# Modulation vectors from raw float32 panels: the conditioning becomes the moving operand

## The chip, the cores and the metric

The kernel runs on one core of a Trainium2 chip. The metric is the device time of one execution in microseconds. The engines of the core work side by side and are kept in step by semaphores: TensorE (PE, its weight loads PEld), VectorE (DVE), ScalarE (ACT), GpSimd (POOL) and SyncE (SP), which issues the transfers here.

## The reference, cut to what matters

Two layers of a diffusion backbone work on 640 tokens, 128 of a prompt and 512 latents. Every layer begins with six modulation vectors of 1024 channels, for the prompt's conditioning and for the latents' apart:

```python
mod = jnp.dot(jax.nn.silu(cvec), w_mod[l]) + b_mod[l]          # w_mod[l]: 1024 x 6144
sh1, sc1, g1, sh2, sc2, g2 = jnp.split(mod[:, None, :], 6, axis=-1)
h = rmsnorm(x, norm1[l]) * (1 + sc1) + sh1
u = h @ w_in[l]                # convolution, recurrence and attention read u; their merge is m
x = x + g1 * (m @ w_out[l])
h2 = rmsnorm(x, norm2[l]) * (1 + sc2) + sh2
...                            # a gated feed-forward on h2, added with g2
```

`cvec` is a row of 1024 numbers; there are two of them, so a vector is a product of 2 x 1024 by 1024 x 1024. All numbers are float32.

## The kernel before, in words

Channels lie on the 128 partitions, tokens along the free axis. The large products need nearly all of float32: weights and activations are split into two parts that the faster format fp32r holds exactly, and three products are summed (`gemm`, L268, for halves of 256 and 384 tokens; `gemm_tm`, L279). A panel of weights (128 x 2048 float32, 1 MB) is loaded into one of two places of `rawt`, which take turns (`load_raw`, L239); `split_cols` makes the parts, a copy on ScalarE (L249) and a subtraction on VectorE (L250), into one of four places of `wR`.

Of layer 0, five vectors are made on TensorE by `modulation` (L356 to L380); the last of layer 0 and all of layer 1 are made on VectorE (`mod_vectors`), which the change leaves alone. A vector has four panels. Each is split like other weights, in two halves. The split conditioning lies in `cpad` with zeros around it, so that a load of 8 columns of it yields 8 rows of results: two parts for two conditionings, for either half of the channels. The panel's parts then move past it, 512 columns a product (L369), 32 products a vector, all summed in one bank of PSUM. ScalarE copies the 8 x 512 sums out (L372), TensorE turns them in four steps (L374), VectorE adds the parts (L376, L379), and `mod_finish` adds the bias and scales (L387 to L392).

Two vectors, 1 and then 0, are made at the program's start; their panels have four places of their own (`stage`). Vector 1 is made first, then come the loads of the stream `x` (L1174, eight tiles of 128 x 640) with the sums of squares (`SqSum`: squares L460 on ScalarE, sums L461 on VectorE), then vector 0. `make_h` turns the sums into 1 / rms (`stat_rstd`: products with ones, L318, five calls for the two halves of the tokens; then turned back, L327) and writes `h` in two parts (L477, L479 on VectorE, L478 on ScalarE), which all products of the layer read. Vectors 2, 3 and 4 are made beside the recurrence of layer 0: `spread` puts one step, a panel, behind every third step of the large products there, and `weave` puts these between the recurrence's own products (L778 for its levels).

The code is written step by step; a scheduler orders each engine's instructions by what is ready and by priority. Loads, splits and what empties PSUM (inside `hp`) go ahead of the rest. Each engine then works through its list in order.

Of the kernel before, what the change touches and what calls it, by code (L numbers as in the profile page):

```python
# [10 lines left out]
F32 = mybir.dt.float32  # L11
# [13 lines left out]
# taps of the convolution beside the making of queries and keys, and beside a tile of scores  # L25
# [4 lines left out]
# columns of the parameter pack  # L30
# [5 lines left out]
# columns of the row pack (one layer)  # L36
# [3 lines left out]
class Arena:  # L40
    """Columns of one tile, given out and taken back in program order; the tile's
    own tracking orders the accesses. The part that has been free longest goes first."""
# [51 lines left out]
def tile_trunk_step(  # L94
# [33 lines left out]
    # ---------------------------------------------------------------- storage  # L128
# [5 lines left out]
    cpad = cpool.tile([P, KD, 12], F32R, name="cpad")  # L134
# [35 lines left out]
    def banks(kind):  # L170
        """Banks for the large products; pairs for scores and levels; the rest."""
# [18 lines left out]
        else:  # L190
            gring.use(singles(0, 1, 2, 4, 5))
            wring.use(pairs(6))
            tring.use(pairs(6))
            mring.use(singles(3))
# [3 lines left out]
    # ---------------------------------------------------------------- helpers  # L198
# [12 lines left out]
    def flat(pair):  # L211
        """The first 640 columns of two banks."""
        return pair.rearrange("p b n -> p (b n)")[:, :NT]
# [11 lines left out]
    def next_t():  # L225
        """For what is done with at once."""
        ctr["t"] += 1
        return ur[:, 3 + ctr["t"] % 2]

    def load_raw(src, n, at=None):  # L230
        """One panel of weights: n columns per partition."""
# [10 lines left out]
    def split_cols(raw3):  # L242
        """Weights [128, K, c] into two parts that float32r holds exactly; list over k of (hi, lo)."""
# [16 lines left out]
    def gemm(wk, ak, hf):  # L260
        """sum_k w_k^T a_k for one half of the tokens; the three products that float32 holds."""
# [9 lines left out]
    def gemm_tm(wk, ak, i):  # L271
        """(token tile i of a)^T w; [128, 256]."""
# [9 lines left out]
    def panel8(src):  # L282
        """A panel [128, 8, 256]: two column tiles, each a list over k."""
# [7 lines left out]
    def panel_wide(src, K):  # L291
        """A panel [128, K <= 4, 512]: four column tiles."""
# [8 lines left out]
    def rsqrt(dst, var, n):  # L301
        """dst = var ** -0.5 for var > 0."""
# [9 lines left out]
    def stat_rstd(s, sl, scale, eps, post=None, ring=None):  # L312
        """s: [128 ch, 640] whose column sums are the squares; 1 / rms of the tokens of sl
        on every partition, in a psum bank."""
# [15 lines left out]
    def streams(sl):  # L330
        """The parts of a slice of tokens that belong to the prompt (0) and to the latents (1)."""
# [6 lines left out]
    # ---------------------------------------------------------------- constants  # L338
# [1116 lines left out]
```

## Time and profile before

| | |
|---|---|
| median of 3 runs | 2509.78 us (2509.27 to 2509.84) |
| profiled execution, first to last instruction | 2509.0 us |
| TensorE busy | 2480.4 us, 99% |
| VectorE busy | 1747.9 us, 70% |
| ScalarE busy | 916.8 us, 37% |
| DMA, mean | 100 GB/s |

The execution that was profiled lies 0.8 us below the median of the runs by its span; that is what the span leaves out and the spread of the runs. In a group of instructions the columns are: line, engine, operation, tiles written and read, shape, count; then busy microseconds and the mean nanoseconds of one; then the idle time of the engine before them and what ended it. In a timeline a row is a merged piece: its start, how long it lasts from the first start to the last end, engine, line, operation, count, and in brackets the idle time before it. TensorE's products overlap, so the distance between two of them is the piece's length less the last one's own duration, divided by the count less one. In a table of stretches each engine's busy time and count stand in the order PE, PEld, DVE, ACT, POOL, and then the granted TensorE clock (1.00 is 2.4 GHz, 0.50 is 1.2 GHz), the share of the DMA engines and GB/s. Before the first clock event of an execution, at about 14.5 us here, the column reads 1.00 whatever the clock was.

### The profile page before, as it was taken

To read this page: it belongs to the slowest core of one execution; us is meant where nothing else is said; L and a number is where in the kernel's file an instruction comes from. 1 tells how busy PE (TensorE), PEld (TensorE's weight loads), DVE (VectorE), ACT (ScalarE), POOL (GpSimd) and SP (SyncE) were. 2 spreads that over 40 slices of the span, in tenths; PEclk is the share of its full clock that TensorE was granted. 3 is DMA by queue.
4 is the path that set the end of the run, shared out by engine and by line. 5 is a ranking of instruction groups with operands and counts; after the bars stand their busy time and mean duration, and the time that the engine had idled before them with its cause. 6 is when DMAs were issued, how large, how long until landed. Compare 5 with 4: busy or idle time off the path is not lost.

```text
span 2509.0 us, 41312 instructions
## 1 busy us (share of the span) xinstructions
PE 2480.4 (99%) x17054; PEld 2393.0 (95%) x17054; DVE 1747.9 (70%) x3570; ACT 916.8 (37%) x1741; POOL 2.6 (0%) x28
## 2 busy tenths in 40 slices
PE   6999999999999999999999999999999999999999
PEld 4999889999999999999999998899999999999999
DVE  8587788685778897767685868885667884444343
ACT  5244565544332422222243445543433242222221
POOL 0000000000000000000000000000000000000000
PEclk8999999999999999999999999999999999999999
DMA  6222111432243354343332222012222412221221
GB/s 268 75 86 92 70 57 57 145 131 103 76 159 112 110 182 154 120 149 135 137 110 77 99 80 77 34 63 73 80 83 71 151 68 68 85 85 68 76 77 59
DMA packets 60492, 251.01 MB, mean 100 GB/s; under 512 B 6416, under 2 KB 18448, under 8 KB 37776
## 3 DMA queue, kind: packets, MB, share of 16 engines
q1 hardware_dynamic: 60304, 248.37, 28.5%
q8 instruction: 134, 2.20, 0.4%
q14 instruction: 54, 0.44, 0.1%
HBM read 230.52 MB, written 17.83 MB: 99 GB/s over the span
## 4 chain that ended last, share of the span: by engine, by line
PE 96%; DVE 2%; DMA 1%; ACT 1%; issue 0%; SPq 0%; DVEq 0%; ACTq 0%
PE psum L268 74%; PE psum L279 9%; PE psum L778 3%; PE psum L988 2%; PE psum L1024 2%; PE psum L987 1%; PE psum L369 1%; PE psum L1016 1%; PE psum L819 1%; DVE wR L250 1%; DMA aF<-in_wmod_dram 1%; PE psum L933 0%; PE psum L834 0%; PE psum L318 0%; PE psum L837 0%
## 5 line engine op out<-in xcount | busy, mean ns | idle before, releaser
L268 PE MATMUL psum<-hR,wR 128*128 128x256 f32 (+1 forms) x8832 | 1342.7, 311 | 3.1 <-ACT hR L478 2.1
L268 PEld LDWEIGHTS psum<-hR,wR 128*128 128x128 f32 x8832 | 1301.7, 190 | 10.9 <-issue 4.4
L250 DVE TENSOR_TENSOR wR<-rawt,wR 128x1024 fp32r<-128x1024 f32 x324 | 395.3, 1223 | 346.0 <-ACT wR L249 345.2
L249 ACT CAST wR<-rawt 128x1024 fp32r<-128x1024 f32 x324 | 338.4, 1047 | 785.6 <-PE psum L268 679.6
L268 PE MATMUL psum<-oR,wR 128*128 128x256 f32 (+1 forms) x4032 | 609.5, 310 | 0.3 <-DVE aF L1138 0.3
L268 PEld LDWEIGHTS psum<-oR,wR 128*128 128x128 f32 x4032 | 592.1, 189 | 3.3 <-DVE aF L1138 0.5
L1138 DVE SCALAR_TENSOR_TENSOR aF<-psum,modd,aF 128x128 f32<-128x128 f32 (+1 forms) x432 | 174.1, 435 | 105.0 <-PE psum L268 102.8
L279 PE MATMUL psum<-wR,hR 128*128 128x256 f32 x1920 | 243.0, 285 | 0.0
L279 PEld LDWEIGHTS psum<-wR,hR 128*128 128x128 f32 x1920 | 233.5, 191 | 3.5 <-issue 2.8
L639 DVE SCALAR_TENSOR_TENSOR aF<-aF,pk 128x655 f32<-128x655 f32 x240 | 214.9, 895 | 2.9
L411 DVE CUSTOM_DVE_ANT_0 aF<-aF 128x1024 f32<-128x1024 f32 x112 | 136.6, 1219 | 0.8
L1335 DVE TENSOR_TENSOR ur<-ur,psum 128x256 f32<-128x256 f32 (+1 forms) x88 | 42.9, 487 | 75.5 <-PE psum L268 75.5
L994 DVE TENSOR_REDUCE small<-psum 128x1 f32<-128x640 f32 (+1 forms) x80 | 56.6, 714 | 45.0 <-PE psum L988 41.0
L254 ACT CAST oR<-ur 128x256 fp32r<-128x256 f32 (+2 forms) x96 | 45.8, 479 | 93.9 <-DVE ur L1335 83.8
L778 PE MATMUL psum<-aF 128*128 128x128 f32 x560 | 78.1, 287 | 0.7 <-ACT aF L766 0.7
L778 PEld LDWEIGHTS psum<-aF 128*128 128x128 f32 x560 | 72.2, 191 | 4.3 <-ACT aF L766 1.6
L567 ACT ACTIVATE ur<-psum 128x256 f32<-128x256 f32 (+1 forms) x104 | 45.3, 436 | 72.3 <-PE psum L268 72.1
L766 ACT COPY aF<-aF 128x640 f32<-128x640 f32 x56 | 43.8, 782 | 72.8 <-DVE aF L782 59.6
L997 ACT ACTIVATE aF<-psum,small 128x640 f32<-128x640 f32 (+1 forms) x80 | 56.6, 711 | 25.8 <-DVE small L995 25.6
L255 DVE TENSOR_TENSOR oR<-ur,oR 128x256 fp32r<-128x256 f32 (+2 forms) x96 | 49.3, 515 | 19.7 <-ACT oR L254 19.7
L568 DVE SCALAR_TENSOR_TENSOR ur<-ur,psum 128x256 f32<-128x256 f32 (+1 forms) x104 | 50.2, 483 | 16.6 <-ACT ur L567 16.5
L369 PE MATMUL psum<-wR,cpad 128*8 128x512 f32 x160 | 46.4, 424 | 11.7 <-ACT wR L249 9.9
(170 smaller groups left out, 1761.6 us busy)
## 6 DMA issues: line engine op xcount, KB each, us to landing
rawt<-in_win_dram SPq DMA_DIRECT2D x64, 1024.0 KB, 4.8
rawt<-in_wfi_dram SPq DMA_DIRECT2D x44, 1024.0 KB, 4.7
aF<-in_wmodT_dram SPq DMA_DIRECT2D x28, 1024.0 KB, 4.8
rawt<-in_wfo_dram SPq DMA_DIRECT2D x20, 1024.0 KB, 4.9
rawt<-in_wmod_dram SPq DMA_DIRECT2D x12, 1024.0 KB, 4.8
rawt<-in_wbr_dram SPq DMA_DIRECT2D x24, 512.0 KB, 3.4
aF<-in_wmod_dram SPq DMA_DIRECT2D x8, 1024.0 KB, 10.5
aF<-in_xT_dram SPq DMA_DIRECT2D x16, 320.0 KB, 6.0
```

Source lines behind the costliest of these rows:

```text
L249: S.copy(hi, raw3)
L250: V.tensor_tensor(out=lo, in0=raw3, in1=f32(hi), op=ALU.subtract)
L268: T.matmul(ps, lhsT=w, rhs=a[:, sl], start=k == 0 and q == 0, stop=k == n - 1 and q == 2)
L279: T.matmul(ps, lhsT=a[:, sl], rhs=w, start=k == 0 and q == 0, stop=k == n - 1 and q == 2)
L369: T.matmul(ps, lhsT=cpad[:, k, 4 - 4 * i : 12 - 4 * i], rhs=w, start=i == 0 and k == 0 and j == 0, stop=i == 1 and k == 7 and j == 1)
L411: V.tensor_tensor_reduce(out=out, in0=w[:, q * 1024 : (q + 1) * 1024], in1=cb[s], scale=1.0, scalar=0.0, op0=ALU.mult, op1=ALU.add, accum_ ...
L568: V.scalar_tensor_tensor(out=dst[:, sl], in0=dst[:, sl], scalar=1.0, in1=ps, op0=ALU.add, op1=ALU.mult)
L639: V.scalar_tensor_tensor(out=accs[j], in0=pads[j][:, t : t + CO], scalar=w(j, t), in1=accs[j], op0=ALU.mult, op1=ALU.add)
L778: T.matmul(ps[:, c // 4, (c % 4) * P : (c % 4 + 1) * P], lhsT=kc[:, c * P : (c + 1) * P], rhs=qm[:, c * nc1 : (c + 1) * nc1], start=True, ...
L994: V.tensor_reduce(out=mx[:, c : c + 1], in_=srcs[c], axis=AX.XY, op=ALU.max)
L997: S.activation(e.rearrange("p (h n) -> p h n", h=2 if i else 1), srcs[c], AF.Exp, bias=mx[:, c : c + 1], scale=0.125, accum_out=sm[:, c : ...
L1138: last = V.scalar_tensor_tensor(out=x[:, ss], in0=ps[:, ss.start - sl.start : ss.stop - sl.start], scalar=g[:, s : s + 1], in1=x[:, ss], o ...
```

## The change

The panels are not split any more. `modulation` takes 128 x 128 pieces of the raw float32 panel as the stationary operand and moves the two columns of the raw conditioning `cs` past them: four tiles of channels by four pieces a panel, 16 products, 64 a vector. The result has its channels on the partitions, so copy, turning and adding of parts fall away; the sums of the two halves of the 1024 inputs stand side by side in PSUM and are added by VectorE in `mod_finish`. `cpad` goes. At the start the loads of the stream and their squares come before both vectors, and the two vectors take turns with two banks of PSUM (the large products have four there instead of five). In the recurrence they keep one bank. The steps are whole panels, as before. Comments are gone too; the diff leaves that out.

```diff
-    cpad = cpool.tile([P, KD, 12], F32R, name="cpad")
+    cs = cpool.tile([P, 2 * KD], F32, name="cs")
...
         else:
-            gring.use(singles(0, 1, 2, 4, 5))
+            gring.use(singles(0, 1, 4, 5))
             wring.use(pairs(6))
             tring.use(pairs(6))
-            mring.use(singles(3))
+            mring.use(singles(2, 3))
...
-    V.memset(f32(cpad), 0.0)
-    cs = small(16)
...
-    S.copy(cpad[:, :, 4:6], csv)
-    V.tensor_tensor(out=cpad[:, :, 6:8], in0=csv, in1=f32(cpad[:, :, 4:6]), op=ALU.subtract)
...
     def modulation(l, v, stage=None):
-        bank = mring.next()
-        ps = bank[:8]
-        for i in range(2):
-            for half in range(2):
-                raw = load_raw(wmod[l, 2 * v + i, half], RAW, None if stage is None else stage[2 * i + half])
-                for q in range(2):
-                    wk = split_cols(raw.rearrange("p (k c) -> p k c", c=512)[:, 2 * q : 2 * q + 2])
-                    for kk in range(2):
-                        k = half * 4 + q * 2 + kk
-                        for j, w in enumerate(wk[kk]):
-                            T.matmul(ps, lhsT=cpad[:, k, 4 - 4 * i : 12 - 4 * i], rhs=w, start=i == 0 and k == 0 and j == 0, stop=i == 1 and k == 7 and j == 1)
-                yield
-        ev = next_t()
-        S.copy(ev[:8, :512], ps)
-        for b in range(4):
-            T.transpose(bank[:, b * 8 : (b + 1) * 8], ev[:8, b * P : (b + 1) * P], ident[:8, :8])
-        mt = small(32)
-        V.tensor_copy(mt, bank[:, :32])
-        m4 = mt.rearrange("p (b g r) -> p g b r", b=4, r=4)
-        dst = modt[l][:, 8 * v : 8 * v + 8, :]
-        V.tensor_tensor(out=dst.rearrange("p (g b) s -> p g b s", b=4), in0=m4[:, :, :, 0:2], in1=m4[:, :, :, 2:4], op=ALU.add)
-        mod_finish(l, v)
+        ps = mring.next()[:, :32].rearrange("p (h j s) -> p h j s", h=2, s=2)
+        for i in range(4):
+            n, half = 2 * v + i // 2, i % 2
+            raw = load_raw(wmod[l, n, half], RAW, None if stage is None else stage[i])
+            w = raw.rearrange("p (k c) -> p k c", c=512)
+            for j in range(4):
+                for k in range(4):
+                    T.matmul(ps[:, half, 4 * (i // 2) + j], lhsT=w[:, k, j * P : (j + 1) * P], rhs=csv[:, 4 * half + k], start=k == 0, stop=k == 3)
+            yield
+        mod_finish(l, v, src=ps)
 
-    def mod_finish(l, v, j=0, n=8):
+    def mod_finish(l, v, j=0, n=8, src=None):
         c = 8 * v + j
         dst = modt[l][:, c : c + n, :]
         bm = pkl(l, PK_BMOD + c, n)
+        if src is not None:
+            V.tensor_copy(dst, src[:, 0])
+            V.tensor_tensor(out=dst, in0=dst, in1=src[:, 1], op=ALU.add)
...
     stages = [stage.ap[:, i * RAW : (i + 1) * RAW] for i in range(4)]
-    drain(modulation(0, 1, stages))
     ssq = af.alloc(NT)
     sq = SqSum(next_u, ssq.ap)
...
-    drain(modulation(0, 0, stages))
+    for v in (1, 0):
+        drain(modulation(0, v, stages))
     for hf in range(2):
         make_h([r.ap for r in xr], sq, 0, 0, hf)
```

How the lists of the engines change is shown at three places. In the changed kernel L318 to L327 keep their numbers; L362 is the new product with the raw panel, L372 to L377 are `mod_finish`, L464 to L466 are `make_h`, L765 is the recurrence's product.

The first is TensorE at the program's start. Outputs are given as partitions x columns, and rows that repeat are counted:

```order
-L369 MATMUL psum<-wR,cpad 8x512 x32
-L374 MATMUL psum<-ident,ur 128x8 x4
 L318 MATMUL psum<-ones,aF 128x64 x5
+L362 MATMUL psum<-cs,aF 128x2 x16
 L327 MATMUL psum<-ident,small 128x128 x2
-L369 MATMUL psum<-wR,cpad 8x512 x32
-L374 MATMUL psum<-ident,ur 128x8 x4
-L268 MATMUL psum<-hR,wR 128x256 x60
+L362 MATMUL psum<-cs,aF 128x2 x112
+L268 MATMUL psum<-hR,wR 128x256 x65
 L327 MATMUL psum<-ident,small 128x128 x3
```

The products of vector 1, which stood ahead of the statistics of the stream (L318), now stand behind them; L318 is the first thing on TensorE. On SP the eight loads of `xT`, which stood between the fourth and the fifth panel of `wmod`, now stand ahead of all eight panels.

The second is VectorE where the modulation hands over to the norm of the stream. Before (`L250` from `aF` splits a panel of the modulation, from `rawt` one of the first large products):

```order
L477 SCALAR_TENSOR_TENSOR ur<-aF,modd_79,psum 128x128
L250 TENSOR_TENSOR wR<-aF,wR 128x1024 x6
L250 TENSOR_TENSOR wR<-rawt,wR 128x1024 x2
L376 COPY small<-psum 128x32
L477 SCALAR_TENSOR_TENSOR ur<-aF,modd_79,psum 128x128
L379 TENSOR_TENSOR modt_77<-small 128x16
L477 SCALAR_TENSOR_TENSOR ur<-aF,modd_79,psum 128x128
L387 TENSOR_TENSOR modt_77<-modt_77,pk 128x16
L250 TENSOR_TENSOR wR<-rawt,wR 128x1024 x2
```

After, without the waits:

```order
L372 COPY modt_77<-psum 128x16
L373 TENSOR_TENSOR modt_77<-modt_77,psum 128x16
L374 TENSOR_TENSOR modt_77<-modt_77,pk 128x16
L466 SCALAR_TENSOR_TENSOR hR<-ur,modt_77,hR 128x128 x2
L464 SCALAR_TENSOR_TENSOR ur<-aF,modd_79,psum 128x128
L466 SCALAR_TENSOR_TENSOR hR<-ur,modt_77,hR 128x128 x3
L464 SCALAR_TENSOR_TENSOR ur<-aF,modd_79,psum 128x128 x4
L250 TENSOR_TENSOR wR<-rawt,wR 128x1024 x2
L466 SCALAR_TENSOR_TENSOR hR<-ur,modt_77,hR 128x128 x4
L250 TENSOR_TENSOR wR<-rawt,wR 128x1024 x2
```

The splits of the modulation's panels are gone, and the four splits of the first two large panels, of which two stood ahead of the copy out of PSUM, all stand behind it and behind the first steps of the norm.

The third is TensorE in the recurrence's first head. Before:

```order
L778 MATMUL psum<-aF 128x128 x5
L369 MATMUL psum<-wR,cpad 8x512 x2
L1032 MATMUL psum<-ident,aF 128x128 x5
L369 MATMUL psum<-wR,cpad 8x512 x6
L268 MATMUL psum<-hR,wR 128x256 x17
```

After:

```order
L765 MATMUL psum<-aF 128x128 x5
L362 MATMUL psum<-cs,rawt 128x2 x16
L268 MATMUL psum<-hR,wR 128x256 x2
L1019 MATMUL psum<-ident,aF 128x128 x5
L268 MATMUL psum<-hR,wR 128x256 x15
```

A panel is one block of 16 products with 2 columns in place of 8 products with 512; eleven of the twelve panels stand so, and one is parted once.

## Rows read from the trace of the kernel before

**Rows 1.** The page: the span, and busy time by engine.
```profile
span 2509.0 us, 41312 instructions
PE 2480.4 (99%) x17054; PEld 2393.0 (95%) x17054; DVE 1747.9 (70%) x3570; ACT 916.8 (37%) x1741; POOL 2.6 (0%) x28
```

**Rows 2.** The page: the chain that ended last, by engine.
```profile
PE 96%; DVE 2%; DMA 1%; ACT 1%; issue 0%; SPq 0%; DVEq 0%; ACTq 0%
```

**Rows 3.** Stretches: the recurrence of layer 0 with the modulation beside it.
```profile
425.00:590.00 165.00, 165.00 (x1119) 150.15 (x1118) 120.45 (x242) 77.31 (x121) 0.00 (x0) 1.00 0.38 131
```

**Rows 4.** Groups of TensorE's instructions by shape, the whole span.
```profile
L369 PE MATMUL psum<-wR,cpad 128*8 128x512 f32 x160 | 46.4, 424 | 11.7 <-ACT wR L249 9.9 <-DVE wR L250 1.6
...
L318 PE MATMUL psum<-ones,aF 128*128 128x64 f32 x60 | 9.6, 297 | 5.0 <-DVE aF L461 4.7 <-DVE small L321 0.2
...
L318 PEld LDWEIGHTS psum<-ones,aF 128*128 128x128 f32 x60 | 8.8, 213 | 6.1 <-DVE aF L461 5.6 <-DVE small L321 0.4
```

**Rows 5.** Timeline of TensorE's products at the full clock, layer 0's recurrence.
```profile
442.50 2.00 PE L369 MATMUL psum<-wR,cpad 128*8 128x512 f32 x8
...
449.62 1.28 PE L778 MATMUL psum<-aF 128*128 128x128 f32 x10
...
533.11 0.41 PE L374 MATMUL psum<-ident,ur 8*128 8x8 f32 x4
```

**Rows 6.** Timeline of TensorE's loads: three at the start, one later.
```profile
12.40 0.13 PEld L369 LDWEIGHTS psum<-wR,cpad 128*8 128x8 f32 x1 [0.30 <-DVE wR L250]
12.83 0.13 PEld L369 LDWEIGHTS psum<-wR,cpad 128*8 128x8 f32 x1 [0.30 <-issue]
...
27.32 1.35 PEld L318 LDWEIGHTS psum<-ones,aF 128*128 128x128 f32 x6 [0.44 <-DVE small L321]
...
823.81 0.75 PEld L318 LDWEIGHTS psum<-ones,aF 128*128 128x128 f32 x6
```

**Rows 7.** Stretches of the start, by the granted clock.
```profile
21.40:24.60 3.20, 0.39 (x4) 0.29 (x4) 2.71 (x11) 3.04 (x8) 0.00 (x0) 1.00 1.01 422
24.80:34.80 10.00, 6.53 (x20) 3.57 (x21) 8.38 (x35) 5.77 (x8) 0.00 (x0) 0.50 1.01 423
35.00:45.00 10.00, 7.09 (x31) 2.29 (x30) 10.00 (x14) 8.42 (x12) 0.00 (x0) 1.00 0.33 107
45.30:51.90 6.60, 5.58 (x26) 5.40 (x26) 6.60 (x24) 2.96 (x9) 0.22 (x2) 0.50 0.95 345
52.10:60.00 7.90, 7.90 (x69) 7.90 (x67) 5.29 (x15) 2.67 (x8) 0.72 (x5) 1.00 0.03 7
```

**Rows 8.** Timeline of the start: the first panels' splits, then TensorE.
```profile
8.79 1.99 ACT L249 CAST wR<-aF 128x1024 fp32r<-128x1024 f32 x2 [4.03 <-DMA aF<-in_wmod_dram]
11.32 1.99 ACT L249 CAST wR<-aF 128x1024 fp32r<-128x1024 f32 x2 [0.53 <-DMA aF<-in_wmod_dram]
...
25.95 1.11 PE L318 MATMUL psum<-ones,aF 128*128 128x64 f32 x4 [4.17 <-DVE aF L461]
...
32.05 9.46 PE L369 MATMUL psum<-wR,cpad 128*8 128x512 f32 x31 [0.70 <-DVE wR L250]
...
44.66 0.82 PE L268 MATMUL psum<-hR,wR 128*128 128x256 f32 x4 [2.08 <-ACT hR L478]
```

**Rows 9.** Groups of the first 60 us: splits, and squares of the stream.
```profile
L250 DVE TENSOR_TENSOR wR<-aF,wR 128x1024 fp32r<-128x1024 f32 x16 | 18.7, 1221 | 4.4 <-ACT wR L249 4.2
...
L460 ACT ACTIVATE ur<-aF 128x384 f32<-128x384 f32 x7 | 3.6, 518 | 0.2
...
L460 ACT ACTIVATE ur<-aF 128x256 f32<-128x256 f32 x7 | 2.9, 409 | 0.1
```

**Rows 10.** 420 to 600 us: ScalarE's splits; panels' issue to landing.
```profile
L249 ACT CAST wR<-rawt 128x1024 fp32r<-128x1024 f32 x41 | 42.0, 1046 | 35.8 <-PE psum L268 24.3 <-PE psum L369 7.0 <-DMA rawt<-in_wmod_dram 2.8
rawt<-in_wmod_dram SPq DMA_DIRECT2D x10, 1024.0 KB, 4.8
```

## The prediction

> **What bounds the kernel now.** I read the page's first part, then the chain of waits, then the stretches with their granted clock. TensorE is busy 99% of the span and VectorE 70% [rows 1]; the chain that ended last is TensorE for 96% [rows 2]. A busy TensorE is modelled, so I look inside the stretch in which layer 0 makes three of the five vectors, beside the recurrence: in 425 to 590 us it is busy 165.0 of 165.0 us at the full clock [rows 3], and its products follow one another at the distance that their columns set [rows 5]. There a microsecond more on TensorE is a microsecond more of the kernel, and a split less on VectorE or ScalarE is worth nothing, unless it was a split that TensorE waited for. The program's first 45 us are different: two vectors stand there alone, TensorE waits for splits and for the first panel, and the clock is at its half level for parts of it [rows 7, 8].
>
> **What the change adds and removes on TensorE.** Before, a vector is 32 products with 512 columns, behind loads of 8 columns. Eight of them take 2.00 us and the last lasts about 0.42: (2.00 - 0.42) / 7 = 0.226 us each at the full clock [rows 4, 5]. So 32 x 0.226 = 7.2 us, and four turnings of 0.07 make it 7.5. After, a vector is 64 float32 products with a 128x128 matrix stationary and 2 columns moving. The trace shows how a float32 product of two raw operands runs: L318 stands 30 times in the program (six calls of five) and 60 times in the trace, as a pair of load and product twice over [rows 4]. So a vector is 128 pairs. The nearest row is L318 itself, a full load with only 64 columns behind it: six loads in 0.75 us at the full clock, the last about 0.19, so (0.75 - 0.19) / 5 = 0.112 us [rows 6]. With 128 columns behind the same load (L778) ten pairs take 1.28 us: again (1.28 - 0.28) / 9 = 0.111 [rows 5]. Half the columns made nothing shorter, so here the load sets the pace, and 2 columns will not make it shorter either. Bounds for a pair: 0.07 us, a turning with 8 columns behind a load of 128 [rows 5], and 0.225 us, L318 at the half clock, six loads in 1.35 us [rows 6]. I take 0.111 at the full clock and 0.215 at the half: 14.2 us or 27.5 us a vector, against 7.5.
>
> **Recurrence, three vectors.** At the full clock 3 x (14.2 - 7.5) = **+20 us**, all on the path, as TensorE has no idle time there [rows 3]. The removed work hides nothing: of 41 ScalarE splits in that stretch 24 go, and as many on VectorE, some 25 and 29 us [rows 9, 10], but ScalarE's 35.8 us of idle time before them went mostly to waiting for TensorE, not the other way [rows 10].
>
> A second cost hangs on the clock. Each panel's 16 products now stand as one block of 32 pairs, 3.6 us of loads with next to no columns. In the first 45 us the clock fell to half behind two stretches: 21.4 to 24.6 us, where TensorE was busy 0.39 of 3.2 us, and 42 to 44.7 us, where it waited for the hand-over [rows 7, 8]. Whether a block of loads counts as work no row shows. If it does not, a block of 3.6 us is as long as those stretches. The price of a fall is that of the second: 6.8 us at half speed, TensorE busy 5.58 of 6.60 in it, so 2.8 us lost [rows 7]. Twelve blocks: from 0 to 12 x 2.8 = 34 us. I take about half of them, **+15 us**.
>
> **The program's start.** Before, the first panel lands at 8.8 us and the next 2.5 us later [rows 8]; the second vector's products end at 32.05 + 9.46 = 41.5 us and the first large product starts at 44.7 [rows 8]. After, the stream (2.6 MB in eight loads) comes first. The panel's 1.05 MB took 2.5 us, so the stream takes some 6.3 us, and it lands where the first panel's data began to flow: about 6.5 to 13 us; the panels follow at 15.4, 17.9, 20.4 and 22.9. SP has no wait of its own in front of the panels but those for its oldest transfers. The squares of the stream are ScalarE's: about 0.47 each, sixteen of them, 7.4 us [rows 9], and they no longer share ScalarE and VectorE with the splits. So the sums are ready at about 14.6 us, against 25.95 before [rows 8]. But on TensorE the statistics (L318) now stand ahead of every panel, so nothing runs there before 14.6. TensorE then is at its half level, as it was before: the first products of 512 columns lie 0.43 us apart, twice 0.226 [rows 5, 6]. Ten L318 at half speed take 2.6 us; the panels begin at 17.3.
>
> From here the whole case hangs on the clock. The clock rose before only behind streams of 256 or 512 columns a product (in 32 to 35 us and in 46.5 to 52 us) [rows 7, 8]; behind the ten L318, loads and 64 columns at a time, it stayed at half [rows 7], though these 3 us are too short to settle it. With 2 columns a load, columns stream for a fiftieth of the time. I take it that the clock **stays at half**: 256 pairs x 0.215 = 55 us, 0.5 for two turnings between, end at 72.8. The panels are never late at that pace: a panel takes 6.9 us of pairs and 2.5 of transfer. Behind the end, three small VectorE steps replace a copy, four turnings and two steps, 0.5 us less; but the four splits of the first weights, of which two lay ahead of the hand-over, now all stand behind it on VectorE, between the steps of the norm: 2 x 1.2 us more [rows 9]. About +1 in all. So the large products start, and everything behind them, (72.8 - 41.5) + 1 = **+32 us** later.
>
> What else moves costs nothing that I can see. The 16 splits of the start go (18.7 us of VectorE [rows 9]), which were the limit there and are no longer. A raw panel now holds its place in the two weight buffers until TensorE has read it, so a panel of large weights in that place comes later. It needs 4.8 us to land [rows 10] and two splits, some 7.5 us, and three steps of large products of 3 to 4 us and as many levels of the recurrence lie between: 10 us or more. Price if that is wrong: 0 to 5 us.
>
> **Sum.** 20 + 15 + 32 = 67 us on a span of 2509.0, and 2509.78 is the median, 0.8 above the span: 2576.
>
> **The Trainium skill** speaks against my price of a pair. After the row (0.112 us with 64 columns behind a full load): "TensorE: Matmul & The Clock Gate", section "Back-to-back issue gap", gives some 60 cycles, about 25 ns, for a product of 1 to 64 columns that stands alone. By it 640 pairs would be 16 us in all and the change a gain; the row, with loads between, is over four times that, and no run here shows products without loads. The same page's Part 1 says that the clock follows how busy TensorE has lately been, and does not say whether loads count; taken so that they do, it gives the first rival.
>
> **Rivals.** *The clock stays up* (loads count as work). At the start it would rise some 3 to 6 us behind 14.6, as in 32 to 35 us; say at 20. By then 12 pairs are done, the other 244 take 27.1 us, end at 47.6: +6 +1. The recurrence is +20 with no falls. 2510 + 27 = 2537. For it: TensorE's queue is never empty in these blocks. Against it: the ten L318. *The clock is at half at the start, but the blocks of the recurrence are too short to bring it down*: 32 + 20 gives 2562. *The load is cheap* (0.07 us a pair, as behind L374): the recurrence is 3 x (9.0 - 7.5) = +4; at the start the panels set the pace, the eighth lands at about 33, end at 34.5, -6. That is 2508, not slower; below 0.06 us a pair it would be faster. Against it stand both float32 rows at 0.11.
>
> **How the numbers follow.** Half clock at the start with falls in the recurrence 0.50, without falls 0.17, clock up 0.26, cheap load 0.05, and 0.02 for worse than all bounds. The forecast is the first, 2576; its own range is 2565 (few falls) to 2598 (32 + 20 + 34 + some of the 5 us). The range has to take in the clock that stays up, so it begins at 2531. Differences of 0.2%, 5 us, are what the measurement can tell: faster 0.02 and same 0.03 (both from the cheap load), slower 0.95.
>
> **What would show it.** The new product's pairs at 0.21 us apart from 17 to 73 us with the clock at 0.5 confirm the start; at 0.11 with the clock at 1.0 from about 20, the first rival. In the recurrence: 32 pairs in 3.6 us a block, and falls of the clock behind blocks; TensorE still busy throughout, and the stretch 20 us longer without the falls. A pair below 0.1 us, or idle TensorE in front of large products whose panel came late, would make the sum wrong.

## The result and the profile after

| | before | after |
|---|---|---|
| median of four runs each, us | 2509.53 | 2578.24 |
| their range, us | 2508.70 to 2509.84 | 2577.18 to 2580.29 |
| span of the profiled execution, us | 2509.0 | 2576.6 |

The changed kernel takes 1.0275 times as long, with a 95% interval of 1.026 to 1.0289. That is 2.8% slower, 68.7 us; the prediction said 2576 us in a range of 2531 to 2598.

The page of the kernel after: span, busy time by engine, the granted clock in 40 slices, and the chain that ended last by engine and line.

```profile
span 2576.6 us, 42085 instructions
PE 2553.1 (99%) x17514; PEld 2493.6 (97%) x17514; DVE 1703.5 (66%) x3528; ACT 875.6 (34%) x1695; POOL 2.2 (0%) x28
PEclk9999999889999999999999999999999999999999
PE 97%; DVE 1%; ACT 1%; issue 0%; DMA 0%; SPq 0%; ACTq 0%
```

Against [rows 1, 2] VectorE is 44 us and ScalarE 41 us less busy, and the kernel is 68 us longer: the relief came where nobody waited for it. TensorE is 73 us busier. The two 8 in the row of the clock are the first place to look; they are the eighth and ninth of 64 us slices, 451 to 580 us, in which the recurrence of layer 0 begins, with the three vectors beside it.

I cut both traces at three marks: the first large product, the first product of the recurrence (L752 before, L739 after) and the start of the recurrence's last turning in layer 0 (L849, L836).

| | before | after | difference |
|---|---|---|---|
| start, to the first large product | 44.66 | 75.03 | +30.4 |
| from there to the recurrence | 377.7 | 376.2 | -1.5 |
| recurrence of layer 0 | 314.4 | 354.4 | +40.0 |
| the rest | 1772.3 | 1771.0 | -1.3 |
| sum | 2509.0 | 2576.6 | +67.6 |

**The start.** The timeline of TensorE after (start and length in us, line, what, how many records; in brackets idle time and who ended it), answering to [rows 8].

```profile
13.87 1.12 PE L318 MATMUL psum<-ones,aF 128*128 128x64 f32 x4 [13.87 <-DVE aF L448]
15.23 1.54 PE L318 MATMUL psum<-ones,aF 128*128 128x64 f32 x6 [0.25 <-DVE small L321]
16.57 6.93 PE L362 MATMUL psum<-cs,aF 128*128 128x2 f32 x32
23.36 0.67 PE L327 MATMUL psum<-ident,small 128*128 128x128 f32 x2
23.82 47.79 PE L362 MATMUL psum<-cs,aF 128*128 128x2 f32 x224
75.03 0.79 PE L268 MATMUL psum<-hR,wR 128*128 128x256 f32 x2 [3.42 <-ACT wR L249]
```

The statistics now come at 13.9 instead of 26 us, as the stream is first, and it does not help: 256 records of the new product stand behind them in one piece, 54.7 us of busy time at 0.214 us each, and the first large product starts 30.4 us later.

**The recurrence.** The two stretches of layer 0's recurrence, before and after (columns: length, busy us and instructions of TensorE, its loads, VectorE, ScalarE, GpSimd, then granted clock, DMA share, GB/s). The third row is a stretch of the start after, the fourth one of the falls.

```profile
422.35:736.74 314.39, 313.50 (x2180) 296.83 (x2179) 223.65 (x456) 137.53 (x230) 0.00 (x0) 1.00 0.34 114
...
451.26:805.67 354.41, 353.52 (x2456) 350.46 (x2455) 197.42 (x432) 113.90 (x203) 0.00 (x0) 0.93 0.30 101
...
24.00:71.00 47.00, 47.00 (x223) 47.00 (x222) 1.82 (x8) 0.00 (x0) 0.00 (x0) 1.00 0.40 150
...
458.42:465.24 6.82, 6.82 (x33) 6.82 (x33) 1.73 (x3) 0.79 (x1) 0.00 (x0) 0.50 0.41 153
```

TensorE is idle for 0.9 us in either recurrence: no panel came late, and all that was added lies on the path. The clock fell from 1.00 to 0.93 on the mean. The trace's record of the granted clock has ten stretches at 0.5 there, 47.8 us in all, and each begins during one of the twelve panels or within 2 us behind its end. In the start stretch the column reads 1.00 only because the record of the clock begins at 79.5 us in this trace; 223 records in 47.00 us, 0.211 each, are the half clock: the second experiment below has the same distance beside a record of 0.50.

Two panels of the recurrence after, one at the full clock and one in which the clock falls, and the large products behind them.

```profile
456.30 4.90 PE L362 MATMUL psum<-cs,rawt 128*128 128x2 f32 x32
461.05 0.78 PE L268 MATMUL psum<-hR,wR 128*128 128x256 f32 x2
...
477.31 3.63 PE L362 MATMUL psum<-cs,rawt 128*128 128x2 f32 x32
480.80 6.01 PE L268 MATMUL psum<-hR,wR 128*128 128x384 f32 x24
...
506.69 4.41 PE L268 MATMUL psum<-hR,wR 128*128 128x384 f32 x24
```

A panel of 32 records takes 3.63 us at the full clock, the last of them some 0.2, so (3.63 - 0.2) / 31 = 0.111 us each; the panel during which the clock falls (at 458.4) takes 4.90. Behind the panel at 477 the same 24 large products take 6.01 us instead of 4.41: the fall at 482.3 lies in them.

### The profile page after: what moved, and what is told of

Its sections match the earlier page's. It is cut to its first block, busy times and chain, and to the rows that moved or that the text cites. A ratio compares the mean times of both kernels' runs of the same rounds, so it can differ in the third digit from the quotient of the medians.

```text
span 2576.6 us, 42085 instructions
## 1 busy us (share of the span) xinstructions
PE 2553.1 (99%) x17514; PEld 2493.6 (97%) x17514; DVE 1703.5 (66%) x3528; ACT 875.6 (34%) x1695; POOL 2.2 (0%) x28
## 4 chain that ended last, share of the span: by engine, by line
PE 97%; DVE 1%; ACT 1%; issue 0%; DMA 0%; SPq 0%; ACTq 0%
PE psum L268 73%; PE psum L279 9%; PE psum L362 4%; PE psum L765 3%; PE psum L975 2%; PE psum L1011 2%; PE psum L974 1%; PE psum L1003 1%; PE psum L806 1%; PE psum L920 0%; PE psum L821 0%; PE psum L318 0%; PE psum L824 0%; PE psum L823 0%; PE psum L739 0%
## 5 line engine op out<-in xcount | busy, mean ns | idle before, releaser
L250 DVE TENSOR_TENSOR wR<-rawt,wR 128x1024 fp32r<-128x1024 f32 x300 | 366.3, 1222 | 354.1 <-ACT wR L249 353.3
L249 ACT CAST wR<-rawt 128x1024 fp32r<-128x1024 f32 x300 | 313.8, 1048 | 788.2 <-PE psum L268 664.9
L765 PE MATMUL psum<-aF 128*128 128x128 f32 x560 | 78.4, 288 | 0.7 <-ACT aF L753 0.7
L765 PEld LDWEIGHTS psum<-aF 128*128 128x128 f32 x560 | 72.6, 193 | 3.8 <-ACT aF L753 1.3
L465 ACT ACTIVATE hR<-ur,modt 128x128 fp32r<-128x128 f32 (+1 forms) x96 | 41.4, 469 | 90.4 <-DVE modt L374 58.7
L555 DVE SCALAR_TENSOR_TENSOR ur<-ur,psum 128x256 f32<-128x256 f32 (+1 forms) x104 | 50.2, 483 | 22.5 <-ACT ur L554 22.4
```

Of the source, the lines that this page charges most:

```text
L249: S.copy(hi, raw3)
L250: V.tensor_tensor(out=lo, in0=raw3, in1=f32(hi), op=ALU.subtract)
L765: T.matmul(ps[:, c // 4, (c % 4) * P : (c % 4 + 1) * P], lhsT=kc[:, c * P : (c + 1) * P], rhs=qm[:, c * nc1 : (c + 1) * nc1], start=True, ...
```

## Theory and rivals

My theory was the prediction's: the new product costs a full load of weights per record whatever its columns, and with 2 columns behind a load the clock goes down. So the loss is one of loads and clock, at the start and in the recurrence each for itself. Rivals: the rate of the new product is slow for another reason than the clock (columns would not help); the clock was merely cold at the start (warming it would help); the order of the start, not the product, is what costs; the recurrence is longer because everything reaches it later.

## Experiments

All times of the table are from the trace of one profiled execution, in us, but the first column of numbers, which is the median of the timed runs. More columns, warm start, half panels, old order and quarter panels have a single timed run each; four runs of the changed kernel lie 3.1 us apart, and each difference read from these five is larger, but for the old order, which is read as none. "At half" is what the record of the clock has at 0.5 inside the recurrence of layer 0.

| kernel | time | first large product | recurrence | at half |
|---|---|---|---|---|
| before | 2509.53 | 44.66 | 314.4 | 0 |
| after | 2578.24 | 75.03 | 354.4 | 47.8 |
| more columns | 2541.35 | 51.22 | 341.1 | 17.1 |
| warm start | 2567.41 | 70.04 | 347.9 | 34.1 |
| half panels | 2561.17 | 74.94 | 336.5 | 6.8 |
| old order | 2576.21 | 75.33 | 351.3 | 41.0 |
| new start alone | 2541.19 | 74.19 | 315.5 | 0 |
| columns and half panels | 2535.85 | 51.1 | 336.5 | 6.8 |
| quarter panels | 2566.32 | 74.5 | 341.5 | 17.1 |
| stream first alone | 2508.21 | 42.86 | 314.5 | 0 |
| vector 1 raw | 2510.05 | 45.63 | 314.5 | 0 |
| stream first, vector 1 raw | 2512.10 | 46.66 | 314.5 | 0 |
| in turns | 2512.68 | 48.15 | 314.5 | 0 |

### More columns behind the same loads

The conditioning vector is repeated along the moving operand, so that each product has 128 columns at the start and 32 in the recurrence; number and order of the loads are those of the changed kernel.

```diff
-        ps = mring.next()[:, :32].rearrange("p (h j s) -> p h j s", h=2, s=2)
+        if stage is None:
+            R, ps = 16, mring.next()
+        else:
+            R, ps = 64, psum[:, 0:4].rearrange("p b n -> p (b n)")
+        ps = ps.rearrange("p (h j r s) -> p h j r s", h=2, j=8, s=2)
...
-                    T.matmul(..., rhs=csv[:, 4 * half + k], ...)
+                    T.matmul(..., rhs=csv[:, 4 * half + k].unsqueeze(1).to_broadcast([P, R, 2]), ...)
...
-        mod_finish(l, v, src=ps)
+        mod_finish(l, v, src=ps[:, :, :, 0])
```

> The changed kernel with the same loads and the same number of products, but more moving columns: the two columns of the conditioning are repeated, to 128 columns at the program's start (four banks of PSUM) and to 32 beside the recurrence (one bank). Theory (a stream of full loads with two columns behind each leaves the clock at half at the start and brings it down in the recurrence): at the start the clock rises 3 to 7 us behind the first product at 14 us, the pairs are then 0.112 us apart, their stream ends at 47 to 49 us instead of 71.6, and the large products begin 23 us earlier; beside the recurrence the pairs stay at 0.11 us and the ten falls of the clock become fewer or none, 0 to 20 us. In all 2533 to 2554 us. Rival one (the clock does not follow the columns; it stays low because nothing dense ran before, or because of the loads): end at 71 us as before, 2577. Rival two (the recurrence's extra time is waiting for raw panels in the two weight buffers): that stretch stays at 354 us.

Measured: 2541.35 us. The start, in TensorE's timeline, then a stretch of it with its clock, and the recurrence:

```profile
18.20 30.36 PE L366 MATMUL psum<-cs,aF 128*128 128x128 f32 x252
51.22 8.62 PE L268 MATMUL psum<-hR,wR 128*128 128x256 f32 x49 [2.66 <-ACT hR L469]
...
22.50:48.50 26.00, 26.00 (x233) 25.87 (x232) 5.30 (x12) 3.98 (x4) 0.00 (x0) 1.00 0.73 273
...
427.39:768.52 341.13, 339.97 (x2456) 336.76 (x2455) 197.49 (x432) 113.76 (x203) 0.00 (x0) 0.97 0.30 105
```

Sixty-four times the columns make the start 23.8 us shorter. The record of the clock stands at full from 22.5 us, a little later than I had said, and 233 records take 26.00 us: 0.1116 us each, the same as with 2 columns at the full clock. So the load sets the pace up to 128 columns, and 23.8 of the 30.4 us that the start had lost were the clock; the other 6.6 are left with the loads at the full clock. In the recurrence, where eleven of the twelve panels still stand whole, 32 columns cut the time at half clock to about a third (17.1 against 47.8 us): four falls, while the same blocks with 2 columns have ten in the changed kernel, nine with the old order and eight with the warm start. The number of falls so differs from one kernel to the next where the recurrence's own products are the same, but not down to four. This rules out that the product is slow for another reason.

### A warm clock ahead of the same records

Twelve float32 products of a matrix of ones, with 512 columns, run on TensorE in the first 14 us, while it waits for data; nothing uses their result.

```diff
     V.memset(ones, 1.0)
+    with hp():
+        for _ in range(12):
+            T.matmul(psum[:, 4], lhsT=ones, rhs=ones.unsqueeze(1).to_broadcast([P, 4, P]), start=True, stop=True)
```

> The changed kernel with twelve products of ones by ones (512 columns each, float32, result unused) ahead of the statistics, from 1 us to about 14 us, where TensorE was idle. Theory: the clock rises behind the first of them and stands at full when the two-column stream begins at 15.5, then falls within some 3 to 7 us of that stream; the stream ends at 64 to 68 us instead of 71.6, 2570 us. Rival (the clock is low in that stream only because TensorE came to it cold): it stays at full, the stream's 256 pairs take 28 us and end at 44, and the kernel takes 2549 us.

Measured: 2567.41 us. TensorE's timeline, then two stretches, of the dense products and of the long block:

```profile
1.05 13.20 PE L344 MATMUL psum<-ones 128*128 128x512 f32 x24 [1.05 <-DVE ones L341]
14.09 0.55 PE L318 MATMUL psum<-ones,aF 128*128 128x64 f32 x4
...
15.61 3.69 PE L365 MATMUL psum<-cs,aF 128*128 128x2 f32 x32
19.16 0.41 PE L327 MATMUL psum<-ident,small 128*128 128x128 f32 x2
19.41 47.21 PE L365 MATMUL psum<-cs,aF 128*128 128x2 f32 x224
...
6.40:14.00 7.60, 7.60 (x19) 3.38 (x18) 6.84 (x27) 6.24 (x16) 0.00 (x0) 1.00 1.02 406
...
20.10:66.50 46.40, 46.40 (x219) 46.40 (x218) 1.82 (x8) 0.00 (x0) 0.00 (x0) 0.50 0.42 157
```

The first 32 records run at 0.11 us, at the full clock that the dense products left. From 20.0 us the clock is at half for 54.6 us, although the record of TensorE is busy 46.40 of 46.40 us, and the other 224 need 0.21 each. The start gains 5 us and no more: the clock was not merely cold, the block itself takes it down. The dense products also show that a record is not always paced by its load: 19 records with 512 columns fill 7.60 us at the full clock, 0.40 us each.

### Half panels in the recurrence

The same product in steps of half a panel, twice as many steps, so that large products come in between.

```diff
             for j in range(4):
                 for k in range(4):
                     T.matmul(...)
-            yield
+                if j % 2:
+                    yield
...
-            if n % 3 == 2:
+            if n % 3:
                 take(other, 1)
```

> The changed kernel with each panel beside the recurrence done in two steps of 8 products, one behind the second and one behind the third of every three steps of large products, so that 20 blocks of 16 pairs (1.75 us) and 2 of 32 stand in place of 11 blocks of 32 and one that is parted. The start is as in the changed kernel. Theory (a block of 3.5 us of loads brings the clock down): the falls become two or none, the recurrence's stretch shortens from 354.4 to 334 to 340 us, the kernel to 2557 to 2563. Rival (the extra 20 us are waits for raw panels, or the loads themselves): 354 us and 2577, or longer, since a panel now holds its place over two steps.

Measured: 2561.17 us, the recurrence 336.5 instead of 354.4. The stretch of the recurrence, and one of the two places in it where two halves came to stand in one piece:

```profile
451.36:787.86 336.50, 335.63 (x2461) 332.82 (x2460) 199.67 (x434) 115.31 (x205) 0.00 (x0) 0.99 0.32 110
...
471.36 1.84 PE L362 MATMUL psum<-cs,rawt 128*128 128x2 f32 x16
473.06 1.31 PE L268 MATMUL psum<-hR,wR 128*128 128x256 f32 x9
...
531.96 3.87 PE L362 MATMUL psum<-cs,rawt 128*128 128x2 f32 x32
535.70 4.52 PE L268 MATMUL psum<-hR,wR 128*128 128x256 f32 x24
```

Two falls are left of ten, 6.8 us, and they begin at 460.1 and 535.2: just behind the first panel (456.2 to 459.8) and at the end of the one at 531.96, the only two that stand whole. With "after", this gives the price of the recurrence: 17.9 us for 41.0 us at half clock, 0.437 us each; and without any fall 336.5 - 0.437 x 6.8 - 314.4 = **19.1 us** for the loads. The 40.0 us of the changed kernel are then 19.1 for loads and 20.9 for the falls. The line was drawn through two kernels; five others of the table test it. It gives 351.4 for the old order (measured 351.3), 348.4 for the warm start (347.9), 341.0 for more columns (341.1), 336.5 for columns and half panels (336.5) and 341.0 for quarter panels (341.5).

### The order of the start put back

Vector 1, the stream, vector 0, as before, with the new product.

```diff
+    drain(modulation(0, 1, stages))
     ssq = af.alloc(NT)
...
-    for v in (1, 0):
-        drain(modulation(0, v, stages))
+    drain(modulation(0, 0, stages))
```

> The changed kernel with the order of the start put back: vector 1, then the stream, then vector 0. Theory (the pairs take 0.2145 us at the half clock wherever they stand): they begin when the first panel lands, at 8.8 us, 64 products end at 36.3, the statistics take 2.6, the other 64 products end at 66.5; the large products begin at 70 instead of 75, and the kernel takes 2572 us. Rival (the stream first is what costs the start, by keeping TensorE idle until 14 us): the start comes back to what it was before, 2548 us.

Measured: 2576.21 us; the first large product at 75.33 instead of 75.03.

```profile
7.98 27.44 PE L362 MATMUL psum<-cs,aF 128*128 128x2 f32 x128 [7.98 <-DMA aF<-in_wmod_dram]
41.48 1.12 PE L318 MATMUL psum<-ones,aF 128*128 128x64 f32 x4 [6.05 <-DVE aF L448]
```

The order costs nothing, and my 70 us was missed as well as the rival's return to before: with the old order the first 128 records begin earlier, at 7.98 us, and run at the price that I had said, 0.214 us, but TensorE then waits 6 us for the stream's squares, which I had left out. What is slow is the 256 records.

### The new start alone, and the order alone

In the first kernel the start is the changed one and the recurrence has the split product of before; in the second only the order is changed, with the split product everywhere. `modulation_raw` is the new product under a name of its own and is not shown again. The new start alone also has the banks of PSUM as the change has them, four for the large products.

```diff
 # new start alone
-    drain(modulation(0, 1, stages))
     ssq = af.alloc(NT)
...
-    drain(modulation(0, 0, stages))
+    for v in (1, 0):
+        drain(modulation_raw(0, v, stages))
```
```diff
 # order alone
-    drain(modulation(0, 1, stages))
     ssq = af.alloc(NT)
...
-    drain(modulation(0, 0, stages))
+    for v in (1, 0):
+        drain(modulation(0, v, stages))
```

> The changed start whole (stream first, both vectors by raw panels with 2 columns), the recurrence with the split product of before. Theory (two separate losses: the start pays for 256 pairs at half clock, the recurrence for its own 384 pairs and the falls that they bring): the first L268-like product stands at 75 us as after, the recurrence lasts 314 us as before, so 2509.5 + 30.4 - 1.5 = 2538 us. Rival (the recurrence is longer because everything reaches it later, or because the clock has been used up ahead): it stays near 350 us and the time near 2577.

> Only the order of the start is changed: x first, then vectors 1 and 0, both by the split product of before. Theory (the first product waits for the 16 splits of 1.2 us on VectorE, whose time beside x is the same in either order): within 4 us, 2505 to 2512. Rival A (putting x first lets VectorE work on the squares while the panels come, and nothing queues behind): first product at 38 to 40 instead of 44.7, 2503 to 2505. Rival B (VectorE stands idle until x is there and has all splits behind it): 2513 to 2516.

Measured: 2541.19 us for the new start (ratio 1.0126, 1.0113 to 1.014), 2508.21 for the order alone (0.9997, 0.9988 to 1.0006; no difference that can be told). The recurrence with the new start:

```profile
452.02:767.56 315.54, 313.81 (x2179) 296.95 (x2178) 223.32 (x456) 137.50 (x230) 0.00 (x0) 1.00 0.33 114
```

It is 315.5 us long, within 1.1 us of before, and the clock never falls in it: it is not longer because it begins later. The new start alone costs 30.1 us of span (29.5 of them ahead of the first large product) and the changed recurrence 40.0; the changed kernel lost 67.6, so the two losses add within 3 us. The time is 3 us over the expected 2538: the 1.5 us that I took off between the first large product and the recurrence did not come back (377.8 us against 377.7 before), and the rest I did not follow. As that stretch did not grow, four banks instead of five cost the large products nothing that shows. With the order alone the first large product comes 1.8 us earlier, less than the timed runs can tell.

### Both remedies together, and smaller pieces

Columns and half panels in one kernel, then quarter panels with 2 columns.

```diff
 # quarter panels, against half panels
-                if j % 2:
-                    yield
+                yield
...
-            if n % 3:
-                take(other, 1)
+            take(other, 2 if n % 3 == 0 else 1)
```

> The changed kernel with 128 moving columns at the start, 32 in the recurrence, and half a panel to a step there. Theory (the losses add: the start 6.6 as with columns alone; the recurrence 19 for the loads at full clock and at most 2 for falls): 2532 to 2535. Rival (32 columns cost time of their own in the recurrence, beside the falls): 2538 or more, above the 22 of the halves with 2 columns.

> The changed kernel with a quarter of a panel (8 pair records) to a step in the recurrence, one or two steps at a time. Theory (the recurrence pays about 19 us for the loads and 0.44 us for each microsecond at the half clock, and the clock falls only behind a panel's records in one piece): no or one fall, the recurrence 333 to 335 us long against 336.5 with halves, 2557 to 2560. Rival (shorter pieces cost time of their own, a change of product each, or the clock falls just as often): 338 us or more, 2562 or more.

Measured: 2535.85 us for both (1.0103, 1.009 to 1.0117), just above the 2532 to 2535 expected: the start +6.5 and the recurrence 336.5, equal to half panels with 2 columns. So 32 columns cost nothing, and remove nothing, where the pieces are already small. This is the best form that I found with all five vectors raw, and it is still 1% slower than before.

The quarter panels missed: 2566.32 us, the recurrence 341.5 instead of 333 to 335. There are three falls, 17.1 us. The order of the program sets steps of 8 records beside each other in places, and there they stand:

```profile
557.45 2.85 PE L362 MATMUL psum<-cs,rawt 128*128 128x2 f32 x24
560.16 1.63 PE L268 MATMUL psum<-oR,wR 128*128 128x256 f32 x6
561.59 1.70 PE L362 MATMUL psum<-cs,rawt 128*128 128x2 f32 x8
...
567.32 1.84 PE L362 MATMUL psum<-cs,rawt 128*128 128x2 f32 x16
569.02 0.63 PE L835 MATMUL psum<-ident,aF 128*128 128x128 f32 x4
569.49 2.79 PE L362 MATMUL psum<-cs,rawt 128*128 128x2 f32 x16
```

The falls begin at 559.9 and 570.2, and the third, at 624.8, behind another piece of 24 records; a fourth such piece, at 530.9, brought none. So the half of my expectation that tied a fall to a whole panel in one piece is wrong: pieces that stand near each other do it too. The price of a microsecond at half clock held (341.0 us by the line above).

### The raw product where VectorE seemed to be the limit

Before, the start waits for splits, so I let the raw product take only vector 1 there, with 128 columns, and left the rest as before: first in the old order, then with the stream first, then with the two vectors' panels in turns. The raw product has four banks of PSUM there, and the split product's bank changes its number; the large products keep five. The diffs show the order alone, of the first and the third kernel.

```diff
 # vector 1 raw
-    drain(modulation(0, 1, stages))
+    drain(modulation_raw(0, 1, stages))
     ssq = af.alloc(NT)
```
```diff
 # in turns
-    drain(modulation(0, 1, stages))
     ssq = af.alloc(NT)
...
-    drain(modulation(0, 0, stages))
+    pairs_, split_ = modulation_raw(0, 1, [stages[1], stages[3]] * 2), modulation(0, 0, [stages[0], stages[2]] * 2)
+    for _ in range(5):
+        take(split_, 1)
+        take(pairs_, 1)
```

> Order of before; at the start vector 1 goes by raw panels with 128 moving columns, vector 0 by the split product; the recurrence by the split product. Theory (the raw product costs 0.12 us a pair record at full clock and takes 8 splits of 1.2 us from VectorE, which bounds the start of before): 128 records behind the loads, done by 27 us, vector 0's 8 splits done by 32, first product at 37 to 41 against 44.7, so 2503 to 2506. Rival (the pairs run at half clock here too, 0.21 us each, and end at 36 with vector 0 queued behind them): first product at 45 to 47, 2509 to 2513.

> Stream first, then vector 1 by raw panels with 128 columns and vector 0 by the split product; the recurrence by the split product. Theory: the pairs begin at 16 us behind the squares, 30 of them at half clock, end at 34; the 32 products of vector 0 behind them take 7 us; first product at 43 to 44, 2508 to 2510. Rival (VectorE, not TensorE, is late, and it is relieved): first product at 38 to 40, 2503 to 2505.

> Stream first; at the start the four panels of vector 0 by the split product and the four of vector 1 by raw panels with 128 columns take turns, panel by panel; the recurrence by the split product. Theory (with vector 1 whole ahead of vector 0 the splits had to wait for free parts behind the raw pairs; in turns VectorE's 8 splits of 1.2 us and TensorE's 128 pair records of 0.12 us run beside each other): TensorE has 15.4 + 6.8 us from 18 us on, first product at 42 to 43.5 against 44.7, 2505 to 2508. Rival (the pairs run at half clock between the slow products, 0.21 us each): first product at 50 or later, 2514 or more.

Measured: 2510.05 us (1.0002, 0.9993 to 1.0011), 2512.10 (1.0012, 1.0004 to 1.0021) and 2512.68 (1.0013, 1.0004 to 1.0022). None is faster, the last two are a tenth of a per cent slower, and all three of my expectations were missed (2503 to 2506, 2508 to 2510 and 2505 to 2508). The first lies in its rival's range, but not for the rival's reason, as the pairs did not run at half clock throughout. They were as cheap as I thought; the rows show what I had left out. First the vector 1 raw kernel, then the one with the stream first, then the one in turns:

```profile
8.20 17.00 PE L391 MATMUL psum<-cs,aF 128*128 128x128 f32 x128 [8.20 <-DMA aF<-in_wmod_dram]
...
21.66 0.17 DVE L401 COPY modt<-psum 128x16 f32<-128x16 f32 x1 [3.00 <-PE psum L391]
...
32.11 9.16 DVE L251 TENSOR_TENSOR wR<-aF,wR 128x1024 fp32r<-128x1024 f32 x8
...
45.63 0.74 PE L269 MATMUL psum<-hR,wR 128*128 128x256 f32 x4 [2.08 <-ACT hR L494]
```
```profile
27.55 1.99 ACT L250 CAST wR<-aF 128x1024 fp32r<-128x1024 f32 x2 [14.51 <-DMA aF<-in_wmod_dram]
...
33.20 2.33 PE L369 MATMUL psum<-wR,cpad 128*8 128x512 f32 x9
...
41.41 2.00 PE L369 MATMUL psum<-wR,cpad 128*8 128x512 f32 x7 [0.28 <-DVE wR L251]
```
```profile
39.77 3.29 PE L391 MATMUL psum<-cs,aF 128*128 128x128 f32 x28
...
42.99 0.41 PE L374 MATMUL psum<-ident,ur 8*128 8x8 f32 x4
...
44.79 2.35 DVE L251 TENSOR_TENSOR wR<-rawt,wR 128x1024 fp32r<-128x1024 f32 x2
...
47.06 0.35 DVE L495 SCALAR_TENSOR_TENSOR hR<-ur,modt,hR 128x128 fp32r<-128x128 f32 x1
47.32 0.86 DVE L493 SCALAR_TENSOR_TENSOR ur<-aF,modd,psum 128x128 f32<-128x128 f32 x3
48.15 1.23 PE L269 MATMUL psum<-hR,wR 128*128 128x256 f32 x4 [4.76 <-ACT hR L494]
```

In the first the pairs are done at 25.2 us, but VectorE's eight splits for vector 0 begin only at 32.1 and end at 41.3, where the last of before's sixteen ended at 40.6: eight splits fewer moved nothing, so the number of splits was not what set that end. Before, vector 1's eight were done at 19.8 us, ahead of the statistics of the stream; only vector 0's eight stand behind these, in both kernels. And the relief is lost ahead of the statistics: VectorE's list has the copy of vector 1's sums (L401) ahead of most of the stream's sums and stands idle for 3.0 us, until the pairs of three panels let it go at 21.7, so the statistics begin on TensorE at 27.2 instead of 25.95 [rows 8], and VectorE's small steps of the statistics and the first two of the norm last until 32.1. This is read from the order in the trace; no run moved L401. With the stream first the pairs end at 33.5 us, as I had said, but vector 0's 32 products behind them take 10.2 us instead of 7, as they wait for splits: the first panel of vector 0 lands only at 27.5, behind vector 1's. In turns, vector 0's last turnings (L374) queue on TensorE behind raw pairs until 43.0, and the next steps of the norm (L495, L493) queue on VectorE behind a split of the first weights, until 47.1: the first large product is 3.5 us late.

## Why the prediction was right, point by point

The range, 2531 to 2598, was wide enough for two of the rivals, so that the time lies in it says little; what bears the prediction out are its terms.

- **A record's price: right.** I took 0.111 us at the full and 0.215 at the half clock from L318 and L778 [rows 5, 6]. The new product has 0.111 (477 us) and 0.211 to 0.214 (the start). The bound from the turnings, 0.07, was not approached. The Trainium skill, "TensorE: Matmul & The Clock Gate", section "LDWEIGHTS (loading the stationary operand)", gives a load its columns over 1.2 in ns, 107 ns for 128; the trace agrees with it within 4% at the full clock (0.111) and not at the half, where a load takes nearly twice that (0.211). The figure of about 25 ns in its section "Back-to-back issue gap", which the prediction weighed, is not what a product costs behind a load of its own here.
- **Recurrence, loads: +20 said, 19.1 measured** with the falls taken out.
- **Recurrence, falls: +15 said, 20.9 measured, and both factors were off.** I took six of twelve panels at 2.8 us; the clock fell behind ten, at 20.9 / 10 = 2.1 us each. The price of a fall came from a stretch of 6.8 us [rows 7], and six of the ten were only 3.4 us long. The two errors went against each other.
- **Start: +32 said, +30.4 measured.** The statistics came at 13.9 (14.6 said), the pairs at 16.6 (17.3), their end at 71.6 (72.8), and the hand-over of 3.4 us is 0.3 longer than before where I had said 1. The choice on which it hung, that the clock stays at half, is borne out by the distance of the records (0.211 us), which the second experiment has beside a recorded 0.50.
- **Not in the sum: -2.8.** Another 1.5 us come back between the first large product and the recurrence, and 1.3 behind it. Before, the first large products ran at half clock for 6.6 us [rows 7]; after, from 75.0 until the record begins at full at 79.5, at most 4.5. That is some 1 us of the first, and it fits that nothing came back with the new start alone, where the record begins at full only 7.5 us behind the first large product. The rest, and the 1.3, I did not follow.
- **A panel that comes late, 0 to 5 us: nothing.** TensorE's idle time in the recurrence is 0.9 us before and after.
- **Rivals.** "The clock stays up" fell for the kernel as changed: it would have ended at 2537. It is what more columns do: 2541, and 2536 with half panels. "Half at the start, no falls", 2562, is nearly the half panels' 2561. So the prices of both came out within a few us, and only the chance was to be settled.
- **Slips of no weight.** The sum, 67 us on 2509.78, is 2577, not 2576. And two columns stream for less than a hundredth of a load's time, not a fiftieth: by [rows 5], 512 take 0.226 us, so two take 0.001 of 0.111.

The forecast of 2576 against 2578 is better than its terms: the recurrence was 5 us more than said, the start and what came back 4 us less.

## What to carry to other kernels

A float32 product of raw operands counts by its loads: two loads of 128 columns each, 0.11 us a load at the full clock, whatever moves behind them up to 128 columns (0.40 us with 512). Turning a wide moving matrix into many stationary ones therefore saves nothing on TensorE, here 14 us a vector instead of 7.5. It could pay only where TensorE waits for the splits that it removes, and no run here shows that it does: three tries at such a place gained nothing. Where such a product must stand, give it columns or part it between dense products, and look at the granted clock of the stretch before the busy share.

## What the runs showed of the hardware

I had not expected that TensorE's record can be busy without a gap while the clock goes down and stays down: 46.40 of 46.40 us at 0.50 with 219 records, each a load with 2 columns behind it, against 26.00 of 26.00 us at 1.00 with 233 records of 128 columns. Nor that a load follows the granted clock as the columns do: 0.111 us at the full level (2.4 GHz) and 0.211 at the half (1.2 GHz), so a block of loads that takes the clock down slows itself.
